# Splitting the keys and queries of a hybrid decoder's attention out of PSUM and stacking them by way of DRAM

## The chip, the cores and the metric

One core of one Trainium2 chip runs the kernel. The metric is the device time of one execution in microseconds, as the median of several runs. A profiled execution gives the trace from which all durations below are read.

## What is computed

One inference step of a decoder trunk of two layers (D_MODEL 1024, 512 prompt rows, and 8 sequences of 4 sample rows against a paged cache). The mixing sub-layer of a layer, cut to what matters:

```python
def hybrid_layer(x, pos, conv_prev, pool_prev, attend, lam_init, p):
    h = rms_norm(x, p['g_mix_pre'])
    z = h @ p['w_in']
    a, ga, u, vb, q, k, v, xd = jnp.split(z, IN_SPLITS, axis=-1)      # 8 x 256 columns
    ya, conv_new = conformer_conv(a, ga, conv_prev, ...)              # 31 taps, LayerNorm, swish
    yb, v_rows = chunk_sgu(gelu(u), gelu(vb), ...)                    # u * (tril(W_s) LN(v) + b)
    o = attend(q, k, v, lam)                                          # softmax 1 - lam * softmax 2
    yc = rms_norm(o, p['attn_sub_g'], LN_EPS) * (1.0 - lam_init)
    yd, pool_new = pool_mix(xd, pool_prev, pos, p['pool_w'], p['pool_scale'])
    x = x + rms_norm(jnp.concatenate([ya, yb, yc, yd], axis=-1) @ p['w_out'], p['g_mix_post'])
    gate, up = jnp.split(rms_norm(x, p['g_ffn_pre']) @ p['w_gu'], 2, axis=-1)
    x = x + rms_norm((silu(gate) * up) @ p['w_down'], p['g_ffn_post'])
    return x, k, v, conv_new, pool_new, v_rows
```

The attention has 4 heads with two softmax maps each (8 maps, 32 dimensions each), a linear position bias per head, and is causal.

## The kernel before

`trunk` runs the two layers one after the other; in each, `mixing` (L348 on) and then the feed-forward part of the prompt, beside which the sample rows' cache attention runs in the background. Every product of the prompt is made from split operands: a float32 value is rounded to a high half, and what is left is the low half; three products (high by high, low by high, high by low) are summed in PSUM.

In `mixing` the input projection has eight column groups of 256, in the order of the list at L395: convolution input, its gate, keys, queries, values, pooling input, u, and the gating's v. A group's 1 MB of raw weights is loaded on SyncE's queue (L198, two buffers); ScalarE casts the high half (`whi`, L190) and VectorE subtracts for the low half (`wlo`, L193). Each group is two features of 128 columns, each feature two halves of the rows: the first 256, and, two steps later, the other 256 and the 32 sample rows. A half is 24 matmuls into the PSUM tile `acc` (two banks), and an eviction by ScalarE. Keys and queries are evicted to `kT` and `qT` (L381); after the second half of the last query feature, `stack` (L459) begins. For each of two chunks `c` (two heads each) it transposes the keys on TensorE for the output, casts the high half on ScalarE (`qkh`, L473) and subtracts on VectorE (`qkl`, L474), and copies pieces of 32 partitions with 12 transfers per stack on SyncE's queue (L478, 48 per layer) into `st_k` and `st_q`. These hold, one under the other, high, low, high of the keys against high, high, low of the queries, so that one matmul of 96 rows makes the three products.

`attention` (L482) is put in after the values. It goes through eight units (row tile i, head hh) in each chunk: two scores matmuls, VectorE's instruction that adds the bias and takes the minimum (L501), ScalarE's exponential with its sum (L503). Three units later come the weights of a unit: a reciprocal (L511), a scaling (L512), the difference of the two maps (L513), transposes on TensorE (L516), their copy (L518), and after each second head the product with the values. Beside it VectorE runs the 60 taps of the convolution (`cacc`, L416), whose norm and transposes (L439, L447, L449) come later. `gating` (L564) begins behind the last eviction: GELU (L586, L587), then per row tile two transposes, statistics and POOL's power for 1/sqrt, the normalised tile (L595) times the gain (L596) plus the bias (L597), then the spatial matmuls and the sum with the spatial bias (L607). `pooling` is at L618. The four results go into the output projection, whose first half of 512 columns starts with the pooling's rows; the second half's weights are cast by ScalarE (L190) behind the last results.

The order on each engine is made when the program is built, by a scheduler that simulates the engines; on the chip each engine and each queue takes its instructions in that order. The tiles `p` (L499, 10 buffers), `t512` (4 buffers) and `y` (4 buffers) are rings.

## Time and profile before

| | us |
|---|---|
| median of 3 runs (lowest to highest) | 1449.32 (1446.21 to 1450.23) |
| the profiled execution | 1448.71 |
| its span | 1446.8 |
| TensorE busy | 1372.0 (95%) |
| VectorE busy | 823.8 (57%) |
| ScalarE busy | 504.7 (35%) |
| GpSimd busy | 262.7 (18%) |

The span is what the trace covers; the execution's own time has 1.9 us around it. PE is TensorE, PEld its weight load, DVE VectorE, ACT ScalarE, POOL GpSimd, SP SyncE. An L number is a line of the kernel. A busy share is an average over stages with different limits, so the rows that follow are read by stage: the mixing of layer 0 lies at about 13 to 192 us, that of layer 1 at about 740 to 907.

### The profile page before, as it was taken

To read this page: it belongs to the slowest core of one execution; us is meant where nothing else is said; L and a number is where in the kernel's file an instruction comes from. 1 tells how busy PE (TensorE), PEld (TensorE's weight loads), DVE (VectorE), ACT (ScalarE), POOL (GpSimd) and SP (SyncE) were. 2 spreads that over 40 slices of the span, in tenths; PEclk is the share of its full clock that TensorE was granted. 3 is DMA by queue.
4 is the path that set the end of the run, shared out by engine and by line. 5 is a ranking of instruction groups with operands and counts; after the bars stand their busy time and mean duration, and the time that the engine had idled before them with its cause. 6 is when DMAs were issued, how large, how long until landed. Compare 5 with 4: busy or idle time off the path is not lost.

```text
span 1446.8 us, 22864 instructions
## 1 busy us (share of the span) xinstructions
PE 1372.0 (95%) x9114; PEld 1078.7 (75%) x9114; DVE 823.8 (57%) x1660; ACT 504.7 (35%) x985; POOL 262.7 (18%) x271
## 2 busy tenths in 40 slices
PE   6999787999999999999989988989999999999997
PEld 6987576877666777777689976777776677768775
DVE  4986759866434333333669976778663333333344
ACT  4346634322224321222343474543322332222231
POOL 1000145455300000000220011544442000000003
PEclk9999799999999999999999997999999999999999
DMA  6452134888848752132434521468877496213132
GB/s 206 116 156 73 59 121 145 301 307 297 296 164 254 241 171 77 59 117 106 150 120 119 146 68 58 163 237 281 318 276 266 153 315 220 81 61 114 59 135 91
DMA packets 160091, 242.15 MB, mean 167 GB/s; under 512 B 10444, under 2 KB 118226, under 8 KB 159986
## 3 DMA queue, kind: packets, MB, share of 16 engines
q1 hardware_dynamic: 141410, 173.32, 37.1%
q0 software_dynamic: 18432, 67.12, 12.4%
q8 instruction: 72, 1.18, 0.3%
q14 instruction: 33, 0.27, 0.1%
q10 hardware_dynamic: 144, 0.26, 0.0%
HBM read 222.33 MB, written 12.04 MB: 162 GB/s over the span
## 4 chain that ended last, share of the span: by engine, by line
PE 81%; DVE 11%; ACT 2%; DMA 2%; issue 2%; POOL 1%; SPq 1%; DVEq 0%; POOLq 0%; ACTq 0%
PE acc L126 61%; PE sx L126 12%; PE ps L126 3%; DVE sca L872 2%; PE s L126 1%; DVE cacc L416 1%; DVE p L501 1%; DVE wlo L193 1%; DVE m L1301 1%; PE oT L126 1%; DVE x_t L1294 1%; ACT whi L190 1%; PE ps L516 1%; SPq L478 1%; PE ps L1001 1%
## 5 line engine op out<-in xcount | busy, mean ns | idle before, releaser
L126 PE MATMUL acc<-xhi,whi 128*128 128x512 f32 (+2 forms) x1152 | 405.5, 353 | 3.2 <-ACT whi L190 2.0
L126 PE MATMUL acc<-xhi,wlo 128*128 128x512 f32 (+2 forms) x1152 | 403.4, 351 | 0.2 <-DVE wlo L193 0.2
L126 PE MATMUL acc<-xlo,whi 128*128 128x512 f32 (+2 forms) x1152 | 402.0, 349 | 1.3 <-DVE xlo L238 1.3
L190 ACT CAST whi<-raw 128x1024 fp32r<-128x1024 f32 x178 | 184.3, 1048 | 333.7 <-PE acc L126 292.8
L193 DVE TENSOR_TENSOR wlo<-raw,whi 128x1024 fp32r<-128x1024 f32 x172 | 217.1, 1268 | 128.7 <-ACT whi L190 126.8
L126 PEld LDWEIGHTS acc<-xhi,whi 128*128 128x128 f32 x1152 | 217.1, 189 | 42.2 <-issue 8.0
L126 PEld LDWEIGHTS acc<-xlo,whi 128*128 128x128 f32 x1152 | 217.2, 189 | 31.9 <-issue 4.1
L126 PEld LDWEIGHTS acc<-xhi,wlo 128*128 128x128 f32 x1152 | 216.9, 188 | 31.5 <-issue 4.7
L126 PE MATMUL acc<-whi,h 128*128 128x512 f32 x704 | 226.7, 397 | 0.0
L126 PEld LDWEIGHTS acc<-whi,h 128*128 128x128 f32 x704 | 131.2, 188 | 44.1 <-issue 11.1
L126 PE MATMUL acc<-wlo,h 128*128 128x512 f32 x352 | 138.6, 395 | 0.0
L1276 POOL TENSOR_TENSOR m<-m,g_g_ffn_post 128x512 f32<-128x512 f32 x14 | 20.1, 1437 | 504.9 <-ACT junk L1275 504.9
L989 DVE STREAM_TRANSPOSE kt<-kr 128x1024 f32<-128x1024 f32 x64 | 78.5, 1233 | 27.6 <-DMA kr<-in_cache_k_dram,ik 23.3
L986 POOL DMA_INDIRECT kr<-in_cache_k_dram,ik x64 | 73.8, 1154 | 100.1 <-DVE kt L989 72.2
L416 DVE SCALAR_TENSOR_TENSOR cacc<-hext,pf,cacc 128x512 f32<-128x512 f32 x120 | 85.4, 747 | 0.6
L1345 DVE SCALAR_TENSOR_TENSOR th<-th,acc 128x512 f32<-128x512 f32 (+1 forms) x46 | 29.9, 649 | 87.2 <-PE acc L126 87.0
L126 PEld LDWEIGHTS acc<-wlo,h 128*128 128x128 f32 x352 | 66.1, 188 | 17.6 <-issue 4.5
L174 POOL TENSOR_TENSOR rsw<-rsw,mhalf 128x1 f32<-128x1 f32 (+2 forms) x62 | 39.1, 636 | 202.9 <-DVE rsw L173 189.4
L1016 POOL DMA_INDIRECT vr<-in_cache_v_dram,iv x64 | 63.2, 988 | 57.0 <-PE sx L126 41.2
L1154 DVE SCALAR_TENSOR_TENSOR sth<-sth,ps 128x64 f32<-128x64 f32 x22 | 4.8, 220 | 86.5 <-ACT sth L1153 86.5
L550 POOL TENSOR_TENSOR rse<-e,mhalf 128x8 f32<-128x8 f32 x4 | 8.5, 2130 | 242.7 <-DVE e L548 242.7
L126 PE MATMUL sx<-vr,pt 128*32 128x256 f32 x512 | 49.3, 381 | 0.0
(401 smaller groups left out, 1864.8 us busy)
## 6 DMA issues: line engine op xcount, KB each, us to landing
raw<-in_w_gu_dram SPq DMA_DIRECT2D x44, 1024.0 KB
raw<-in_w_down_dram SPq DMA_DIRECT2D x20, 1024.0 KB
rws<-in_w_gu_dram SPq DMA_DIRECT2D x40, 512.0 KB
raw<-in_w_in_dram SPq DMA_DIRECT2D x16, 1024.0 KB
raw<-in_w_out_dram SPq DMA_DIRECT2D x8, 1024.0 KB
rwo<-in_w_out_dram SPq DMA_DIRECT2D x16, 512.0 KB
rws<-in_w_down_dram SPq DMA_DIRECT2D x16, 512.0 KB
x<-x_t SPq DMA_DIRECT2D x12, 512.0 KB
```

Of the source, the lines that this page charges most:

```text
L126: T.matmul(out, lhsT, rhs, start=start, stop=stop)
L174: G.tensor_tensor(y, v, mhalf[:P, :n], op=ALU.pow)
L190: S.copy(hi, src)
L193: eng.tensor_tensor(lo, src, hi.bitcast(F32), op=ALU.subtract)
L416: V.scalar_tensor_tensor(a, hext[c][:, t:t + SEQ], pf[:, 8 + 2 * t + c:9 + 2 * t + c], a, op0=ALU.mult, op1=ALU.add)
L478: SY.dma_start(s[32 * g:32 * g + 32, jj, :].bitcast(F32), (hi, lo)[seqs[g]][32 * jj:32 * jj + 32, :].bitcast(F32))
L872: V.scalar_tensor_tensor(a[:, c], ext[:, c, :, t:t + 4], pf[:, 8 + 2 * t + c:9 + 2 * t + c], a[:, c], op0=ALU.mult, op1=ALU.add)
L986: G.indirect_dma_start(out=kr, out_offset=None, in_=ck, in_offset=bass.IndirectOffsetOnAxis(ap=ik[:, s, bg:bg + 1], axis=0))
L989: V.transpose(kt, kr)
L1016: G.indirect_dma_start(out=v.rearrange("p t e -> p (t e)"), out_offset=None, in_=cv, in_offset=bass.IndirectOffsetOnAxis(ap=iv[:, s, a:a + ...
L1276: (V if (t, half) == (3, 1) else G).tensor_tensor(m[t][:, hs], m[t][:, hs], gain[:, hs], op=ALU.mult)
L1345: V.scalar_tensor_tensor(th[:, :n], th[:, :n], 0.5, ou[:, :n], op0=ALU.mult, op1=ALU.mult)
```

## The change

Keys and queries are no longer evicted as float32. `ev_qk` writes the high half straight from PSUM (ScalarE) and the low half from PSUM minus that (VectorE), each as 256 columns, into tiles that live through the stage; the queries' scale is in both. `stack(c)` is called at the end of each query feature: on GpSimd's queue it writes both halves of keys and of queries to DRAM and reads each stack back with three transfers (20 per layer; SyncE's 48 go). The output of the keys (`keys_out`) is made by two matmuls with a rounded identity, one for each half, in place of a transpose. `attention` is put in after the first query feature, with gates: a chunk begins when its queries are done, products with the values when those are done. The reciprocal and the scaling of two heads become one instruction each. In `gating` the gain is applied after the spatial matmuls, and the bias goes through the spatial weights once, in four matmuls, into the spatial bias. The ring of `p` has 8 buffers in place of 10, `t512` 3 in place of 4; two small tiles `cn` use the ring `pt`.

```diff
@@ -36,7 +36,7 @@
 URG = 1000
-PB = 10
+PB = 8
 UL = 3
...
@@ -149,6 +149,8 @@
     ident = cst[:, C_ID:C_ID + 128]
+    identr = cp.tile([128, 128], F32R, name="identr")
+    S.copy(identr, ident)
...
+        SY.dma_start(rows[71:73, :], A["sgu_ln_g"][l].rearrange("(c p) -> c p", p=128))
...
+        V.tensor_copy(pf[:, 77:79], o[:, 71:73])
...
-        kT, kh, kl, qh, ql = {}, {}, {}, {}, {}
+        qk = {(nm, c): [mp.tile([128, SEQ], F32R, name=f"{nm}{c}{s}") for s in "hl"] for nm in "kq" for c in range(2)}
+        pb = mp.tile([128, SEQ], F32, name="pb")
+        SY.dma_start(pb, A["c_pbias"])
+        done = set()
...
-        def ev_tmp(d, c, f, tag):
+        def ev_qk(nm, c, f):
+
             def ev(o, half):
-                if half == 0:
-                    d[c] = mp.tile([128, SEQ], F32, tag="p", bufs=PB, name=tag)
+                hi, lo = qk[nm, c]
                 hs = slice(256 * half, 256 * half + 256)
-                if tag == "kT":
-                    S.copy(d[c][:, hs], o[:, :256])
+                if nm == "k":
+                    S.copy(hi[:, hs], o[:, :256])
+                    V.tensor_tensor(lo[:, hs], o[:, :256], hi[:, hs].bitcast(F32), op=ALU.subtract)
                 else:
-                    S.activation(d[c][:, hs], o[:, :256], AF.Copy, scale=cst[:, C_QS + c:C_QS + c + 1])
+                    sc = cst[:, C_QS + c:C_QS + c + 1]
+                    S.activation(hi[:, hs], o[:, :256], AF.Copy, scale=sc)
+                    V.scalar_tensor_tensor(lo[:, hs], o[:, :256], sc, hi[:, hs].bitcast(F32), op0=ALU.mult, op1=ALU.subtract)
                 if half == 1:
-                    S.activation(zs[:, f, :], o[:, 256:288], AF.Copy, scale=1.0 if tag == "kT" else -QSCALE)
+                    S.activation(zs[:, f, :], o[:, 256:288], AF.Copy, scale=1.0 if nm == "k" else -QSCALE)
             return ev
 
-        qT = {}
         order = [
             (0, [(0, ev_copy(hext[0], 0, 0.5, 30)), (1, ev_copy(hext[1], 1, 0.5, 30))]),
             (256, [(2, ev_ga(0)), (3, ev_ga(1))]),
-            (1280, [(10, ev_tmp(kT, 0, 10, "kT")), (11, ev_tmp(kT, 1, 11, "kT"))]),
-            (1024, [(8, ev_tmp(qT, 0, 8, "qT")), (9, ev_tmp(qT, 1, 9, "qT"))]),
+            (1280, [(10, ev_qk("k", 0, 10)), (11, ev_qk("k", 1, 11))]),
+            (1024, [(8, ev_qk("q", 0, 8)), (9, ev_qk("q", 1, 9))]),
...
-        def stack():
+        def stack(c):
+
+            for nm, seqs in (("k", (0, 1, 0)), ("q", (0, 0, 1))):
+                via = dp.tile([2, 128, SEQ], F32, name=f"via{l}{c}{nm}")
+                for i in range(2):
+                    G.dma_start(via[i], qk[nm, c][i].bitcast(F32))
+                st = ST[nm, c] = yp.tile([128, 4, SEQ], F32R, tag="y", name=f"st_{nm}")
+                for g in range(3):
+                    G.dma_start(st[32 * g:32 * g + 32].bitcast(F32), via[seqs[g]].rearrange("(j p) t -> p j t", p=32))
+
+        def keys_out():
             for c in range(2):
-                st = ST[c] = {}
-
                 o = ps()
                 for t in range(4):
-                    T.transpose(o[:, 128 * t:128 * t + 128], kT[c][:, 128 * t:128 * t + 128], ident)
-                kt = mp.tile([128, 4, 128], F32, tag="t512", bufs=4, name="ktok")
+                    for s in range(2):
+                        mm(o[:, 128 * t:128 * t + 128], qk["k", c][s][:, 128 * t:128 * t + 128], identr, start=(s == 0), stop=(s == 1))
+                kt = mp.tile([128, 4, 128], F32, tag="t512", bufs=3, name="ktok")
                 S.copy(kt, o.rearrange("p (t f) -> p t f", t=4))
                 SY.dma_start(O[2][l, 0].rearrange("(t p) h c d -> p t (h c d)", p=128)[:, :, 128 * c:128 * c + 128], kt)
                 yield
-                for nm, src, seqs in (("k", kT[c], (0, 1, 0)), ("q", qT[c], (0, 0, 1))):
-                    hi = mp.tile([128, SEQ], F32R, tag="t512", bufs=4, name="qkh")
-                    lo = mp.tile([128, SEQ], F32R, tag="t512", bufs=4, name="qkl")
-                    S.copy(hi, src)
-                    V.tensor_tensor(lo, src, hi.bitcast(F32), op=ALU.subtract)
-                    s = yp.tile([128, 4, SEQ], F32R, tag="y", name=f"st_{nm}")
-                    for jj in range(4):
-                        for g in range(3):
-                            SY.dma_start(s[32 * g:32 * g + 32, jj, :].bitcast(F32), (hi, lo)[seqs[g]][32 * jj:32 * jj + 32, :].bitcast(F32))
-                    st[nm] = s
-                    yield
 
         def attention():
-            pb = mp.tile([128, SEQ], F32, tag="pb", name="pb")
-            SY.dma_start(pb, A["c_pbias"])
             y = None
             for c in range(2):
-                st = ST[c]
+                while ("q", c) not in done:
+                    yield
...
-                        mm(sp[:, :W], st["q"][0:96, 2 * hh + m, 128 * i:128 * i + 128], st["k"][0:96, 2 * hh + m, 0:W])
+                        mm(sp[:, :W], ST["q", c][0:96, 2 * hh + m, 128 * i:128 * i + 128], ST["k", c][0:96, 2 * hh + m, 0:W])
...
-                    V.reciprocal(dn[:, 2:3], dn[:, 1:2])
-                    V.tensor_scalar(dn[:, 3:4], dn[:, 0:1], dn[:, 2:3], nlam, op0=ALU.mult, op1=ALU.mult)
+                    if hh == 0:
+                        d2 = den[:, i]
+                        V.reciprocal(d2[:, :, 2:3], d2[:, :, 1:2])
+                        V.scalar_tensor_tensor(d2[:, :, 3:4], d2[:, :, 0:1], nlam, d2[:, :, 2:3], op0=ALU.mult, op1=ALU.mult)
...
                         if hh == 1:
+                            while "v" not in done:
+                                yield
                             values(i)
...
-            gr = mp.tile([128, 2, 256], F32, tag="sgr", name="sgr")
-            SY.dma_start(gr[:, 0, :], A["sgu_ln_g"][l, :].partition_broadcast(128))
-            SY.dma_start(gr[:, 1, :], A["sgu_ln_b"][l, :].partition_broadcast(128))
+            gr = mp.tile([128, 256], F32, tag="sgr", name="sgr")
+            SY.dma_start(gr, A["sgu_ln_b"][l, :].partition_broadcast(128))
...
             SG[l] = (wc, bc)
+            o = acc()
+            for h in range(4):
+                mm(o[64 * (h % 2):64 * (h % 2) + 64, 128 * (h // 2):128 * (h // 2) + 128], gr[:, 64 * h:64 * h + 64], wt[:, h, :])
+            V.tensor_tensor(bsg, o[:, :256].rearrange("p (c t) -> p c t", c=2), bsg, op=ALU.add)
             yield
...
                 V.tensor_scalar(vn[:, t, :], o[:, :256], mean, r, op0=ALU.subtract, op1=ALU.mult)
-                V.tensor_tensor(vn[:, t, :], vn[:, t, :], gr[:, 0, :], op=ALU.mult)
-                V.tensor_tensor(vn[:, t, :], vn[:, t, :], gr[:, 1, :], op=ALU.add)
                 yield
...
-                V.tensor_tensor(t, o.rearrange("p (n t) -> p n t", n=4),
-                                bsg[:, c:c + 1, :].to_broadcast([128, 4, 128]), op=ALU.add)
+                V.scalar_tensor_tensor(t, o.rearrange("p (n t) -> p n t", n=4), pf[:, 77 + c:78 + c],
+                                       bsg[:, c:c + 1, :].to_broadcast([128, 4, 128]), op0=ALU.mult, op1=ALU.add)
...
-                if c0 == 1024 and i == 1:
-                    active.append(stack())
+                if c0 == 1024:
+                    done.add(("q", i))
+                    stack(i)
+                    if i == 0:
+                        active.append(attention())
+                    else:
+                        active.append(keys_out())
                 if i == "v":
-                    active.append(attention())
+                    done.add("v")
```

On VectorE, layer 0, around the first score. L501 (L507 after) is the score's minimum, L416 (L425) a tap into an accumulator `cacc`, L193 (L195) a weight low half, L474 an old low half, L399 a query's new one. Before:

```order
L474 TENSOR_TENSOR qkl<-qT,qkh 128x512
L416 SCALAR_TENSOR_TENSOR cacc_800<-hext_232,pf_82,cacc_800 128x512
L416 SCALAR_TENSOR_TENSOR cacc_442<-hext_231,pf_82,cacc_442 128x512
L416 SCALAR_TENSOR_TENSOR cacc_800<-hext_232,pf_82,cacc_800 128x512
L193 TENSOR_TENSOR wlo<-raw,whi 128x1024
L416 SCALAR_TENSOR_TENSOR cacc_442<-hext_231,pf_82,cacc_442 128x512
L416 SCALAR_TENSOR_TENSOR cacc_800<-hext_232,pf_82,cacc_800 128x512
L501 ISA p,mn<-s,pb 128x128
L501 ISA mn 128x1
```

After:

```order
L425 SCALAR_TENSOR_TENSOR cacc_456<-hext_233,pf_84,cacc_456 128x512
L425 SCALAR_TENSOR_TENSOR cacc_831<-hext_234,pf_84,cacc_831 128x512
L195 TENSOR_TENSOR wlo<-raw,whi 128x1024
L399 SCALAR_TENSOR_TENSOR q1l<-acc,cst,q1h 128x256
L425 SCALAR_TENSOR_TENSOR cacc_831<-hext_234,pf_84,cacc_831 128x512
L507 ISA p,mn<-s,pb 128x128
L507 ISA mn 128x1
```

The first score stands behind nine taps more, and q1l, the other chunk's low half, stands ahead of it too.

On GpSimd's queue, layer 0, from the end of the rows' clearing to the attention norm's power (L550, L560). Before, no transfer stands there:

```order
L356 MEMSET dext_233 128x15
L355 MEMSET hext_232 128x30
L356 MEMSET dext_234 128x15
L550 TENSOR_TENSOR rse<-e_1534,mhalf 128x8
L578 AFFINE_SELECT wt<-wt 128x512
```

After (the eight rows for the keys of chunk 0 and the first of chunk 1 stand ahead of these):

```order
L473 DMA via00q<-q0h 128x512
L476 DMA st_q<-via00q 32x4x512 x2
L476 DMA st_k<-via01k 32x4x512 x2
L473 DMA via00q<-q0l 128x512
L476 DMA st_k<-via01k 32x4x512
L476 DMA st_q<-via00q 32x4x512
L473 DMA via01q<-q1h 128x512
L473 DMA via01q<-q1l 128x512
L476 DMA st_q<-via01q 32x4x512 x3
L560 TENSOR_TENSOR rse<-e_1368,mhalf 128x8
```

The read of chunk 0's query stack stands behind writes and reads of chunk 1's keys, and the last third of it behind the write of q0l.

On TensorE, layer 0, around the last matmul of the input projection (`acc<-xhi,wlo 128x288`). L439 and L447 are transposes of the convolution's norm, L516 (L524) of the attention weights, L575 of the spatial weights, L593 of the gating's v. Before:

```order
L126 MATMUL acc<-xhi,wlo 128x288
L126 MATMUL s<-st_k,st_q 128x384 x2
L575 MATMUL acc<-cst,wn 128x128 x4
L439 MATMUL ps<-cst,cacc_442 128x128
L439 MATMUL ps<-cst,cacc_800 128x128
L126 MATMUL s<-st_k,st_q 128x384 x2
L593 MATMUL acc<-cst,uv 128x128 x4
L126 MATMUL s<-st_k,st_q 128x512 x2
L439 MATMUL ps<-cst,cacc_442 128x128
```

After, where the last 96 matmuls of the projection begin at the end of these rows:

```order
L126 MATMUL s<-st_k,st_q 128x512
L126 MATMUL oT<-pt,vtok 64x128
L524 MATMUL ps<-cst,p 128x128 x2
L448 MATMUL ps<-cst,cacc_456 128x128
L448 MATMUL ps<-cst,cacc_831 128x128
L126 MATMUL oT<-pt,vtok 64x128
L126 MATMUL s<-st_k,st_q 128x512
L448 MATMUL ps<-cst,cacc_456 128x128
L448 MATMUL ps<-cst,cacc_831 128x128
L524 MATMUL ps<-cst,p 128x128 x2
L126 MATMUL acc<-wn,pw 128x512
L126 MATMUL acc<-xhi,whi 128x256
```

Chunk 1's widest scores were behind the projection's last matmul and are ahead of its last 96 now.

## Rows read from the trace of the kernel before

**Rows 1.** The page's head: the span and its instructions.

```profile
span 1446.8 us, 22864 instructions
```

**Rows 2.** Layer 0 windows: us, busy PE, PEld, DVE, ACT, POOL; PEclk, DMA share, GB/s.

```profile
40.40:81.00 40.60, 38.92 (x306) 38.21 (x304) 38.75 (x57) 14.09 (x30) 0.00 (x0) 1.00 0.41 116
81.00:130.00 49.00, 45.29 (x325) 40.05 (x325) 43.79 (x120) 27.55 (x77) 0.00 (x0) 0.97 0.42 122
130.00:145.00 15.00, 15.00 (x124) 14.69 (x124) 5.31 (x12) 9.05 (x16) 2.66 (x1) 1.00 0.27 88
145.00:175.30 30.30, 19.48 (x125) 13.58 (x123) 23.67 (x79) 21.36 (x42) 6.91 (x9) 0.66 0.20 68
175.30:190.00 14.70, 13.21 (x66) 10.80 (x64) 5.96 (x12) 4.32 (x7) 2.70 (x4) 1.00 0.01 5
```

**Rows 3.** The same of layer 1's tail.

```profile
862.00:889.60 27.60, 20.13 (x112) 13.53 (x112) 22.81 (x77) 18.53 (x39) 5.09 (x9) 0.63 0.21 74
889.60:905.00 15.40, 13.91 (x80) 11.49 (x76) 6.02 (x12) 4.50 (x7) 2.60 (x4) 1.00 0.02 7
```

**Rows 4.** DVE groups, layer 0: shapes xcount | busy us, mean ns | idle.

```profile
L416 DVE SCALAR_TENSOR_TENSOR cacc<-hext,pf,cacc 128x512 f32<-128x512 f32 x60 | 42.6, 747 | 0.3
L193 DVE TENSOR_TENSOR wlo<-raw,whi 128x1024 fp32r<-128x1024 f32 x16 | 19.8, 1237 | 8.5 <-ACT whi L190 8.4
L512 DVE TENSOR_SCALAR den<-den,lam 128x1 f32<-128x1 f32 x16 | 4.0, 266 | 0.1
L511 DVE RECIPROCAL den<-den 128x1 f32<-128x1 f32 x16 | 2.4, 157 | 5.9 <-ACT p L503 5.9
L595 DVE TENSOR_SCALAR vn<-acc,ag,rsw 128x256 f32<-128x256 f32 x4 | 2.1, 538 | 0.0
L597 DVE TENSOR_TENSOR vn<-vn,sgr 128x256 f32<-128x256 f32 x4 | 1.7, 417 | 0.1
L474 DVE TENSOR_TENSOR qkl<-kT,qkh 128x512 fp32r<-128x512 f32 x2 | 1.4, 688 | 0.7 <-DMA st_q<-qkh 0.7
```

**Rows 5.** DVE timeline (start us, us): eleven taps, and each layer's first score.

```profile
65.40 7.37 DVE L416 SCALAR_TENSOR_TENSOR cacc<-hext,pf,cacc 128x512 f32<-128x512 f32 x11
...
81.05 0.29 DVE L501 CUSTOM_DVE_ANT_0 p<-s,pb 128x128 f32<-128x128 f32 x1 [0.21 <-PE s L126]
...
800.35 0.28 DVE L501 CUSTOM_DVE_ANT_0 p<-s,pb 128x128 f32<-128x128 f32 x1
```

**Rows 6.** Gathered cache keys, 512 KB each: issue ns min/median/max; landing.

```profile
L986 POOL DMA_INDIRECT kr<-in_cache_k_dram,ik x64: 933/941/1936, 252.2 to 1086.2; - x64
...
DMA to landing us min/median/max: 4.2/6.5/9.8
```

**Rows 7.** Query stack: issue ns; PE's waits (us, times, longest); scores.

```profile
L478 SPq DMA_DIRECT2D st_q<-qkh x32: 507/588/1712, 74.3 to 819.0; - x32
...
PE s L126 <- DMA st_q<-qkl: 0.9, 2, 0.7
...
L126 PE MATMUL s<-st_k,st_q 96*128 96x384 f32 x8 | 2.7, 374 | 1.5 <-DVE mn L501 1.4
...
L126 PE MATMUL s<-st_k,st_q 96*128 96x512 f32 x8 | 4.5, 628 | 0.0
```

**Rows 8.** PE timeline: each layer's last projection matmul, output projection's second half.

```profile
144.71 0.29 PE L126 MATMUL acc<-xhi,wlo 128*128 128x288 f32 x1
...
192.29 0.50 PE L126 MATMUL acc<-whi,yd 128*128 128x512 f32 x1 [2.13 <-ACT whi L190]
...
861.56 0.30 PE L126 MATMUL acc<-xhi,wlo 128*128 128x288 f32 x1
...
907.40 0.61 PE L126 MATMUL acc<-whi,yd 128*128 128x512 f32 x1 [2.15 <-ACT whi L190]
```

**Rows 9.** ACT, 130 to 193: table loads (group), weight casts (timeline).

```profile
L503 ACT ACT_TABLE_LOAD x3 | 3.8, 1283 | 0.1
...
188.36 3.88 ACT L190 CAST whi<-raw 128x1024 fp32r<-128x1024 f32 x4
```

More of the change, by code (lines that the diff above doesn't have):

```diff
@@ L277, in params @@
         lam_init = 0.8 - 0.6 * math.exp(-0.3 * l)
-        rows = tp.tile([72, 128], F32, tag="prow", name="prow")
+        rows = tp.tile([74, 128], F32, tag="prow", name="prow")
         for i, n in enumerate(("conv_b", "conv_ln_g", "conv_ln_b", "pool_scale")):
@@ L564, in gating @@
         def gating():
-            wn = mp.tile([128, 4, 128], F32, tag="t512", bufs=4, name="wn")
+            wn = mp.tile([128, 4, 128], F32, tag="t512", bufs=3, name="wn")
             SY.dma_start(wn, A["sgu_w"][l].rearrange("h t s -> t h s"))
```

14 lines of the change are left out of this document (7 added, 7 removed).

## The prediction

> **What bounds the kernel now.** I read the span first [rows 1], then busy time by stage of each mixing sub-layer [rows 2, 3], then VectorE (DVE) by groups and in order of time [rows 4, 5], then the transfers and what waits for them [rows 6, 7], and last the two ends that matter on TensorE (PE) and ScalarE (ACT) [rows 8, 9]. Only the two mixing sub-layers change, some 170 us each. Their middle has three parts. From the gated convolution input to the first attention score (40.4 to 81.0 in layer 0) PE and DVE are both full: 38.9 and 38.8 of 40.6 us [rows 2]. From there to the last matmul of the input projection (145.0, [rows 8]) PE is still nearly full (45.3 of 49.0, then 15.0 of 15.0). Then comes a tail in which nobody is full: from 145.0 to 175.3 PE is busy 19.5 of 30.3 us and its granted clock is 0.66, between its two levels; DVE is busy 23.7 and ACT 21.4. The tail ends when the second half of the output projection starts, at 192.29 in layer 0 and 907.40 in layer 1: 47.3 and 45.5 us after the last projection matmul (144.71 + 0.29; 861.56 + 0.30) [rows 8]. So DVE limits the first part, PE the second, and a chain through ACT, DVE and PE the third.
>
> **The first part gets longer.** In DVE's order the first score now stands behind 50 of the 60 convolution taps in layer 0 and 53 in layer 1, not 41, and behind all eight low-half instructions of keys and queries, where two were. DVE had no slack there, so each of these counts. A tap costs 0.67 us start to start (7.37 us for 11, [rows 5]): 9 x 0.67 = 6.0 us in layer 0, 12 x 0.67 = 8.0 in layer 1. A low half is now a 128x256 instruction that reads PSUM, eight times. The nearest rows are 0.54 us (128x256 from PSUM, L595) and 0.42 (two SBUF operands, L597), and as a lower bound half of the old 128x512 one, 0.34 [rows 4]; I take 0.48, so 8 x 0.48 = 3.8 us (2.8 to 4.3), less the two old ones that stood before the score, 2 x 0.69 = 1.4. Sum: first score **+8.4 us in layer 0 (81.05 to 89.5), +10.4 in layer 1 (800.35 to 810.8)**. ACT's side only gets lighter (the high half is now the copy out of PSUM itself, four casts of 128x512 go); it was busy 14 of 40.6 us, so I price that at nothing.
>
> **The transfers.** 48 copies on SyncE's (SP's) queue go, at 0.588 us of issue each, 28 us per layer [rows 7]. PE waited in the whole front half for these copies twice, 0.9 us in all [rows 7], and for no weight load; what hides the issues is that weights are loaded two tiles ahead. Price 0 (a gain of 0.9 at most). In their place stand 20 transfers of 256 KB on GpSimd's (POOL's) queue, each read behind its write. POOL is idle there (0.00 busy in the first two stretches, [rows 2]) and nothing else of the mixing is queued behind them before the attention norm's power, which ran after 130 us. The path that counts is the last query half of chunk 0: between it and the score stand 13 taps, a weight low half (1.24, [rows 4]) and one low half more, 13 x 0.67 + 1.24 + 0.48 = 10.4 us, so DVE finishes it at 89.5 - 10.4 = 79.1. Then come issue, write, issue, read. No such transfer is in the trace; the nearest is POOL's gather of 512 KB: 0.94 us to issue, 4.2 / 6.5 / 9.8 us to landing (least, median, most, [rows 6]). Halves of 256 KB with plain rows should be near the least: 79.1 + 2 x (0.94 + 4.2) = 89.4, just before DVE gets to the score at 89.5. At the median 94.0, at the most 100.6. I take the least, and keep the others for the rivals. The Trainium skill, "DMA: Bandwidth & Descriptors", section "Anatomy of one DMA — SWDGE (gpsimd) path", gives about 2.0 us plus bytes over 436 GB/s, an estimate of 2.6 us for such a transfer, and says that the receipt of a write to DRAM is the heaviest; by it the stack would be there well before DVE. The trace's least landing of twice the bytes, 4.2 us, is not far from that, its median is.
>
> The same page, section "Issuing engines are not separate DMA queues", speaks against the move: another issuing engine saves only the time of issuing. The rows above agree, in that PE waits for no weight.
>
> **The second part.** From the first score to the last projection matmul PE has the same dense matmuls in both orders. Chunk 1's eight widest scores (four of 384 columns, four of 512) stood behind the last dense one in both layers and stand before it now: 4 x 0.374 + 4 x 0.628 = 4.0 us ([rows 7]; 3.0 if all were as the narrower), and with them four transposes of the convolution's norm, 4 x 0.13 = 0.5. The keys' 16 product matmuls in place of 8 transposes: 306 dense matmuls in 38.9 us are 0.127 each at twice the columns [rows 2], so eight more are 0.5 to 1.0; I take 0.8. Against that stand the 3.7 us in which PE idled from 81 to 130; with fewer taps between the scores I let 3 of them go (0 to 3.7). Net +2.3. Last dense matmul: 145.0 + 8.4 + 2.3 = **155.7** in layer 0; 861.9 + 10.4 + 2.3 = **874.6** in layer 1.
>
> **The tail gets shorter.** DVE's work from first score to 190 was 43.8 + 5.3 + 23.7 + 6.0 = 78.8 us [rows 2]. Of that 9 x 0.75 = 6.7 has moved ahead. The sixteen reciprocals and scalings, 16 x (0.157 + 0.266) = 6.8, become eight of each kind on two heads at about the same duration, 3.4: -3.4. The eight gain and bias steps of 0.42 (L597 and its twin) go, -3.3, and one 128x256 addition comes, +0.4. Two old low halves go, -1.4. Left: 78.8 - 6.7 - 3.4 - 2.9 - 1.4 = 64.4. Between first score and last dense matmul DVE worked 49.1 of 64 us, 0.77; over the new 66.2 us (89.5 to 155.7) that is 50.8, so 13.6 us are left for the tail, where 23.7 + 6.0 = 29.7 were: **-16.1**. Of what is taken out of the tail, chunk 1's scores, exponentials and weights, which stood ahead of the gating on both engines, are the larger part. ACT also had table loads of 1.283 us each in it [rows 9], because the exact GELU alternated with the exponentials: 6 in layer 0's mixing and 4 in layer 1's, one in each after: -6.4 and -3.8. If all of both is on the path, the tail is 47.3 - 16.1 - 6.4 = 24.8 in layer 0; with the table loads hidden, 31.2. For layer 1 (28.8 us of DVE in its tail, [rows 3]; the same removals) 45.5 - 16.1 - 3.8 = 25.6, or 29.4. What is late next is the gating: last eviction, GELU, then four transposed tiles, each through statistics and POOL's power, the spatial matmuls, the product, and on ACT the cast of the result ahead of four weight casts (3.88 us, [rows 9]) that the second output half waits for. Adding that chain up in the new order from rows of the same kind gives 27.5 us, inside both pairs of bounds, and I take it for both. The fold's four extra matmuls (under 1 us) lie where PE idles. Second half of the output projection: 155.7 + 27.5 = **183.2** (192.3 before, -9.1) and 874.6 + 27.5 = **902.1** (907.4, -5.3).
>
> PE will idle some 8 and 10 us in gaps before the first score. In the tail before, where PE was busy 64% of the time, the granted clock was 0.66 [rows 2]; if the gaps do the same to about 10 us of matmuls, a quarter of that is lost in all: +2.5 for both layers (0 to 6). Sum: -9.1 - 5.3 + 2.5 = -11.9 on the profiled 1448.71 us (span 1446.8, the rest lies around it), 1436.8; that run is 0.6 below the median of the runs, so **1437.4**.
>
> **The rivals.**
> 1. *A larger gain.* The gating's chain overlaps more: tail 20 us instead of 27.5, -15 in all, **1422.4**. For it: DVE has only 13.6 us of work left in 27.5. Against: the chain of four tiles through POOL is serial, and the last tile's transposes now stand behind 19 matmuls of the output projection.
> 2. *Landing at the median.* The first score comes 4.5 us later than DVE could take it (94.0), in each layer: **1446.4**, which can no longer be told from no change. DVE takes its instructions in order, so the taps behind that score wait too, and nothing is won back.
> 3. *Both a median landing and a tail whose table loads were hidden* (31 us, so 3.5 more each): 1446.4 + 7 = **1453.4**, still no change that can be measured.
> 4. *Slower: the way through DRAM decides.* Weight loads keep the DMA engines 41% busy in this stretch [rows 2] and the writes and reads are in one POOL queue, each read waiting for its write with the next writes behind it. At landings of 9.8 us, the most in [rows 6], the first score is at 100.6, 11.1 later than in the sum, and 2 x 11.1 = 22.2 more gives **1459.6**. It decides from the point where the added wait per layer passes the gain, 11.9 / 2 = 6 us: a first score later than about 95.5.
> 5. *The change doesn't do what it says:* the queue that it relieves held nobody up. That I have priced in; the gain then comes from attention's earlier place and the lighter DVE alone.
>
> **How the numbers follow.** Forecast (1430 to 1444) 0.41; larger gain 0.13; median landing 0.11; both 0.13; slower 0.22. About 0.3% (4.3 us) is what a measurement of this kernel can tell from no change: faster is below 1445, slower above 1453.7. Rivals 2 and 3 lie between, and the forecast and the first rival below: faster 0.54, same 0.24, slower 0.22. The range reaches from the larger gain to the slow case, 1421 to 1460; cases beyond either end are left some 0.2 in all.
>
> **What would show it.** Right: the first score at about 89 and 811, released by DVE and not by a DMA; the last projection matmul near 156 and 875; one table load in each mixing; the second output half near 183 and 902; transfers on POOL's queue that land in 4 to 5 us; gaps on PE at 74 to 89 ended by DVE's weight low halves. Wrong: PE or DVE waiting at the first score for the read of the query stack (rivals 2 and 4); the tail still above 40 us, with DVE idle in it, which would mean that the chain and not the work set it; or SP's relief showing as earlier weights.

## The result and the profile after

The changed kernel takes 1470.86 us (median of 4 runs, 1470.22 to 1471.66) against 1449.76 for the kernel before (four runs now; 1449.32 was the median of the first three): a ratio of 1.0155, with an interval of 1.0137 to 1.0174. It is 1.5% slower where 0.8% faster was forecast, and it lies outside the range, whose upper end was 1460.

The page's head and the windows of the changed kernel follow, cut where the prediction cut them: from the convolution's start to the first score, from there to the last projection matmul, from there to the output projection's second half. Columns are as in [rows 2]; layer 0 comes first, then layer 1.

```profile
span 1468.5 us, 22838 instructions
...
40.40:90.20 49.80, 39.86 (x294) 38.60 (x292) 45.42 (x70) 11.82 (x25) 9.64 (x17) 0.93 0.54 154
90.20:167.80 77.60, 70.50 (x496) 62.56 (x496) 53.95 (x151) 42.60 (x116) 5.53 (x8) 0.91 0.26 83
167.80:195.10 27.30, 24.53 (x163) 19.04 (x162) 17.89 (x37) 15.19 (x25) 10.71 (x10) 0.94 0.27 83
...
764.30:814.20 49.90, 40.76 (x296) 39.49 (x295) 47.69 (x71) 11.83 (x25) 9.49 (x17) 0.93 0.53 149
814.20:892.00 77.80, 71.44 (x499) 62.90 (x499) 51.57 (x148) 42.63 (x116) 5.50 (x8) 0.91 0.28 86
892.00:922.30 30.30, 25.00 (x161) 19.52 (x159) 19.35 (x37) 15.86 (x27) 11.41 (x10) 0.89 0.35 112
```

The same cut of the kernel before:

```profile
41.20:81.00 39.80, 38.12 (x299) 37.41 (x298) 37.95 (x54) 14.09 (x30) 0.00 (x0) 1.00 0.42 118
81.00:145.00 64.00, 60.29 (x447) 54.75 (x447) 49.10 (x131) 36.60 (x93) 2.66 (x1) 0.97 0.39 114
145.00:192.30 47.30, 32.85 (x190) 24.39 (x188) 30.60 (x91) 27.98 (x51) 11.91 (x14) 0.78 0.16 51
...
760.40:800.40 40.00, 38.61 (x304) 37.90 (x302) 38.18 (x53) 14.09 (x30) 0.00 (x0) 1.00 0.42 119
800.40:861.90 61.50, 58.05 (x447) 53.51 (x448) 49.36 (x133) 36.33 (x93) 2.56 (x1) 1.00 0.40 118
861.90:907.40 45.50, 34.39 (x189) 25.12 (x187) 29.89 (x90) 25.43 (x49) 10.09 (x14) 0.77 0.15 53
```

| us more than before | layer 0 | layer 1 | forecast, 0 / 1 |
|---|---|---|---|
| first part, to the first score | +10.0 | +9.9 | +8.4 / +10.4 |
| second part, to the last projection matmul | +13.6 | +16.3 | +2.3 / +2.3 |
| tail, to the output projection's second half | -20.0 | -15.2 | -19.8 / -18.0 |
| from there to the feed-forward's first gated product | -1.9 | -0.6 | 0 |
| feed-forward to the next layer, or to the end | +3.0 | +7.4 | 0 |

With the start 0.8 us earlier the column sums to the +21.7 of the spans. PE was idle 19.9 us of layer 0's three parts before (1.7, 3.7, 14.5) and is idle 19.8 after (9.9, 7.1, 2.8): the tail's idle time was emptied, and as much of it stands in the two parts ahead.

PE's waits that carry this: the first score of each layer, the last projection matmul, the first matmul of the output projection's second half (start us, us, what ended the idle time before it).

```profile
89.68 0.66 PE L126 MATMUL s<-st_k,st_q 96*128 96x128 f32 x2 [4.73 <-DMA st_q<-via00q]
...
167.46 0.29 PE L126 MATMUL acc<-xhi,wlo 128*128 128x288 f32 x1
...
195.14 0.40 PE L126 MATMUL acc<-whi,yd 128*128 128x512 f32 x1
...
813.77 0.61 PE L126 MATMUL s<-st_k,st_q 96*128 96x128 f32 x2 [1.89 <-issue]
...
891.70 0.30 PE L126 MATMUL acc<-xhi,wlo 128*128 128x288 f32 x1
...
922.30 0.40 PE L126 MATMUL acc<-whi,yd 128*128 128x512 f32 x1
```

They answer to [rows 8]. In layer 1 the profile puts the wait down to "issue", but the read of the last part of the query stack is issued on GpSimd's queue at 805.97 and lands 7.7 us later, at 813.7, just before the score starts. So in both layers the first score came with that read. DVE (the last low half of chunk 0's queries, then twelve taps, then the first score) and POOL's queue (the write of that half, the read behind it) over the same time in layer 0, and last the read of layer 1:

```profile
76.34 0.47 DVE L399 SCALAR_TENSOR_TENSOR q0l<-acc,cst,q0h 128x256 fp32r<-128x256 f32 x1
76.73 8.03 DVE L425 SCALAR_TENSOR_TENSOR cacc<-hext,pf,cacc 128x512 f32<-128x512 f32 x12
...
90.16 0.29 DVE L507 CUSTOM_DVE_ANT_0 p<-s,pb 128x128 f32<-128x128 f32 x1 [3.21 <-PE s L126]
```

```profile
79.76 0.56 POOL L473 DMA_DIRECT2D via00q<-q0l  x1
80.31 0.56 POOL L476 DMA_DIRECT2D st_k<-via01k  x1
85.61 0.55 POOL L476 DMA_DIRECT2D st_q<-via00q  x1 [4.74 <-DMA via00q<-q0l]
...
805.97 0.55 POOL L476 DMA_DIRECT2D st_q<-via10q  x1
```

The half is done at 76.8, but its write is issued only at 79.76, behind a read of q0h that waited for its own write; it lands before 85.61, and the read is in at 89.7. That is 12.9 us from the finished half to the score on PE, and DVE waits 3.21 us of them. In layer 1 it is 11.4 us (802.4 to 813.8), and DVE waits 0.56.

Where the second part grew: busy time of PE in it, by tile, layer 0, before and after (the columns after the length are PE and PEld, then the other engines that touch the tile). First `acc`, `s` and `ps` before:

```profile
81.00:145.00 64.00, 48.84 (x340) 44.07 (x340) 0.00 (x0) 7.03 (x21) 0.97 0.39 114
...
81.00:145.00 64.00, 6.88 (x25) 4.22 (x25) 15.23 (x35) 0.00 (x0) 0.97 0.39 114
...
81.00:145.00 64.00, 6.43 (x42) 4.88 (x42) 0.76 (x2) 3.73 (x9) 0.97 0.39 114
```

The same three after:

```profile
90.20:167.80 77.60, 51.52 (x341) 46.37 (x342) 0.00 (x0) 7.02 (x21) 0.91 0.26 83
...
90.20:167.80 77.60, 10.65 (x31) 5.67 (x30) 19.91 (x43) 0.00 (x0) 0.91 0.26 83
...
90.20:167.80 77.60, 12.53 (x72) 9.58 (x72) 4.58 (x10) 6.27 (x16) 0.91 0.26 83
```

The dense matmuls (`acc`) are as many, but take 2.7 us more at the lower granted clock (0.91 for 0.97); scores take 3.8 us more, transposes and other small products (`ps`) 6.1 us more (72 for 42), products with the values 1.1 us more (52 for 40). Matmuls of different tiles overlap, so these add up to more than the 10.2 us by which PE's busy time grows. Its idle time grows from 3.7 to 7.1.

### The profile page after: what moved, and what is told of

Its sections match the earlier page's. It is cut to its first block, busy times and chain, and to the rows that moved or that the text cites. A ratio compares the mean times of both kernels' runs of the same rounds, so it can differ in the third digit from the quotient of the medians.

```text
span 1468.5 us, 22838 instructions
## 1 busy us (share of the span) xinstructions
PE 1385.7 (94%) x9146; PEld 1090.9 (74%) x9146; DVE 819.2 (56%) x1624; ACT 491.1 (33%) x972; POOL 279.2 (19%) x311
## 4 chain that ended last, share of the span: by engine, by line
PE 77%; DVE 11%; DMA 4%; issue 4%; ACT 2%; POOL 2%; SPq 0%; DVEq 0%; POOLq 0%; ACTq 0%
PE acc L126 59%; PE sx L126 11%; PE ps L126 3%; DVE sca L888 2%; DVE cacc L425 2%; DVE wlo L195 2%; PE s L126 1%; DMA kr<-in_cache_k_dram,ik 1%; DVE m L1317 1%; DVE x_t L1310 1%; PE oT L126 1%; ACT whi L192 1%; PE ps L1017 1%; PE ps L524 1%; PE ps L237 1%
## 5 line engine op out<-in xcount | busy, mean ns | idle before, releaser
L126 PE MATMUL acc<-xhi,whi 128*128 128x512 f32 (+2 forms) x1152 | 410.2, 357 | 6.5 <-ACT whi L192 3.2
L126 PE MATMUL acc<-xhi,wlo 128*128 128x512 f32 (+2 forms) x1152 | 407.7, 354 | 4.0 <-DVE wlo L195 4.0
L126 PE MATMUL acc<-xlo,whi 128*128 128x512 f32 (+2 forms) x1152 | 406.6, 353 | 1.1 <-DVE xlo L240 1.1
L195 DVE TENSOR_TENSOR wlo<-raw,whi 128x1024 fp32r<-128x1024 f32 x172 | 216.4, 1264 | 151.6 <-ACT whi L192 138.3
L126 PEld LDWEIGHTS acc<-xhi,whi 128*128 128x128 f32 x1152 | 222.0, 193 | 47.3 <-issue 8.7
L126 PEld LDWEIGHTS acc<-xhi,wlo 128*128 128x128 f32 x1152 | 221.9, 193 | 35.4 <-issue 4.9
L126 PEld LDWEIGHTS acc<-xlo,whi 128*128 128x128 f32 x1152 | 221.7, 192 | 32.7 <-issue 4.8
L425 DVE SCALAR_TENSOR_TENSOR cacc<-hext,pf,cacc 128x512 f32<-128x512 f32 x120 | 84.2, 744 | 0.8
L126 PE MATMUL sx<-kt,qs 128*32 128x128 f32 x1024 | 45.2, 281 | 0.2 <-DVE kt L1005 0.2
```

The lines of the kernel that those rows point to most:

```text
L126: T.matmul(out, lhsT, rhs, start=start, stop=stop)
L195: eng.tensor_tensor(lo, src, hi.bitcast(F32), op=ALU.subtract)
L425: V.scalar_tensor_tensor(a, hext[c][:, t:t + SEQ], pf[:, 8 + 2 * t + c:9 + 2 * t + c], a, op0=ALU.mult, op1=ALU.add)
```

## The experiments

All ratios are to the kernel before, run on the same chip.

**Run e1** asks why the last 96 projection matmuls stand behind chunk 1. In the trace of the changed kernel the pooling's second product is the last thing ahead of them, and its additions on DVE (L643) stand behind the last score:

```profile
147.63 1.38 DVE L643 TENSOR_TENSOR wn<-s 64x512 f32<-64x512 f32 x2
```

```profile
149.85 0.69 PE L448 MATMUL ps<-cst,cacc 128*128 128x128 f32 x2 [3.44 <-DVE xn L450]
151.16 0.69 PE L524 MATMUL ps<-cst,p 128*128 128x128 f32 x2 [0.62 <-DVE xn L450]
151.64 1.91 PE L126 MATMUL acc<-wn,pw 128*128 128x512 f32 x2
152.56 1.20 PE L126 MATMUL acc<-xhi,whi 128*128 128x256 f32 x1
```

```diff
-                o = acc()
+                o = ps()
                 mm(o, pw[:, c, :], wn[:, 0:SEQ])
```

> The changed kernel with one edit: the pooling's product goes to the PSUM ring of the small tiles (ps, three buffers) instead of the ring that the input projection uses (acc, two buffers). Theory A (the pooling's tile stands in the projection's ring, its VectorE additions stand behind chunk 1's scores, so the last 96 projection matmuls wait for it): the last projection matmul comes back from 167.9 to 155-159 in layer 0 and from 892 to 876-882 in layer 1, no idle of TensorE over 1 us between 135 and 155, and the time is 1446-1458. Theory B (the chain of chunk 1's scores itself, in TensorE's order, holds the projection up): the ends stay within 3 us of 167.9 and 892, the time at 1466-1472. Theory C (the longer first part, first score at 90 and 814, is the loss): time stays over 1464 too.

1485.64 us, ratio 1.0211 (1.0174 to 1.0248). The three windows of layer 0:

```profile
40.60:91.90 51.30, 39.85 (x294) 38.58 (x292) 45.40 (x70) 11.82 (x25) 9.66 (x17) 0.92 0.56 157
91.90:152.30 60.40, 60.30 (x459) 56.80 (x458) 41.08 (x113) 36.51 (x98) 3.33 (x4) 0.95 0.32 99
152.30:198.30 46.00, 33.36 (x198) 24.06 (x198) 28.84 (x75) 24.32 (x46) 10.85 (x14) 0.89 0.12 39
```

Theory A's place is right: with the tile elsewhere PE is idle 0.1 us in the second part, which ends at 152.3 instead of 167.8. Its price is wrong: the tail is 46.0 us again, and the kernel is no faster (1.0211 where the changed kernel had 1.0155; the two intervals just touch). The wait on the pooling is real, and what it held back was not the limit; attention's rest, now behind the projection, took the time back.

**Run e2** puts attention where it was, with all else as changed.

```diff
-                    if i == 0:
-                        active.append(attention())
-                    else:
+                    if i == 1:
                         active.append(keys_out())
                 if i == "v":
                     done.add("v")
+                    active.append(attention())
```

> The changed kernel with attention put in after the values, as before, everything else of the change kept (halves from PSUM, way through DRAM, batched reciprocals, folded gain and bias). Theory A (attention's earlier place pushes the pooling's additions back on VectorE): chunk 1's scores are again among and behind the last projection matmuls, the last of them comes at 150-158 in layer 0, time 1440-1456. Theory C (the way through DRAM and the eight low halves in the first part cost the time): the first part is as long as in the changed kernel, time 1462-1472.

1471.81 us, ratio 1.0124 (1.0087 to 1.0162). The first score comes at 100.8 and 816.3. The early place is not the cause of the loss; the rest of the change is about as slow without it (the interval overlaps that of the changed kernel, 1.0137 to 1.0174).

**Runs e3 and e4** make two small edits in the kernel before: the fold of gain and bias with the batched reciprocals (their hunks of the change), and e1's edit.

> The kernel before with only the batched reciprocals and the folded gain and bias of the gating: some 6.3 us less of VectorE's work per layer, all of it between the first score and the output projection. If VectorE's work sets the tail: 1436-1444. If the gating's chain through ScalarE and GpSimd sets it: 1445-1451.

> The kernel before with the pooling's product in the ring of the small tiles. Before, the pooling was done at 129, ahead of the last 96 projection matmuls, and TensorE idled 3.7 us from 81 to 130. Theory A expects a small effect here, 1443-1451; a gain over 8 us would mean that the ring was already the limit before.

e3: 1450.83 us, ratio 0.998 (0.9963 to 0.9997). e4: 1449.44 us, ratio 0.9971 (0.9953 to 0.9989). Both are worth a little. DVE's removed work, some 6 us per layer, buys 1 to 1.5 us in each (0.2% of the kernel), as expected where a chain sets the tail and not DVE's work.

**Runs e5, e6 and e7** take the change apart. e5 is the changed kernel with direct copies; e6 is the kernel before with attention's early place alone; e7 is the kernel before with the way through DRAM alone.

The edit of e5, in `stack(c)` of the changed kernel (e7 makes the opposite one in the kernel before):

```diff
-                via = dp.tile([2, 128, SEQ], F32, name=f"via{l}{c}{nm}")
-                for i in range(2):
-                    G.dma_start(via[i], qk[nm, c][i].bitcast(F32))
                 st = ST[nm, c] = yp.tile([128, 4, SEQ], F32R, tag="y", name=f"st_{nm}")
-                for g in range(3):
-                    G.dma_start(st[32 * g:32 * g + 32].bitcast(F32), via[seqs[g]].rearrange("(j p) t -> p j t", p=32))
+                for jj in range(4):
+                    for g in range(3):
+                        SY.dma_start(st[32 * g:32 * g + 32, jj, :].bitcast(F32), qk[nm, c][seqs[g]][32 * jj:32 * jj + 32, :].bitcast(F32))
```

The edit of e6, in the kernel before, cut to where the parts are put in; the gates in `stack` and `attention` are those of the change:

```diff
-                if c0 == 1024 and i == 1:
-                    active.append(stack())
+                if c0 == 1024:
+                    active.append(stack(i))
+                    if i == 0:
+                        active.append(attention())
                 if i == "v":
-                    active.append(attention())
+                    done.add("v")
```

> The changed kernel with the stacks filled by 48 direct copies on SyncE's queue again, from the new halves, no way through DRAM and nothing on GpSimd's queue; all else as changed. Theory D (the first part's new idle of TensorE, 8 us per layer, comes from the way through DRAM and is not won back): first score at 81-86 in layer 0, TensorE's idle before it under 4 us, time 1452-1463. Theory E (what the first part loses the second would have lost, TensorE's work and idle are only moved): 1466-1473. If SyncE's issues delayed the weights, TensorE would wait for weight halves before 81 and the time would be above 1473.

> The kernel before with only attention's place changed: the stack is made chunk by chunk (old copies on SyncE's queue, from the old evictions), attention is put in after the first query feature, with the same gates. In its order all of chunk 1's scores stand ahead of the last 96 projection matmuls, as in the changed kernel, and the table loads fall from 11 to 5. Theory F (the early place only moves TensorE's work and idle from the tail into the second part): the last projection matmul 8-15 us later in layer 0 than the 145.0 of before, the tail from there to the output projection's second half 28-38 instead of 47.3, time 1443-1456. If the early place is by itself what made the changed kernel slow: over 1460. If it is a gain that something else ate: under 1440.

> The kernel before with only the way of the stacks changed: two writes to DRAM and three reads for each on GpSimd's queue in place of twelve copies on SyncE's. In its order the first score stands behind 52 taps instead of 41 and behind 54 more projection matmuls. Theory D: the first score comes at 88-96 instead of 81.05 and the time is 1453-1466. If the way through DRAM is hidden (attention has slack there): 1446-1452.

e5: 1459.15 us, ratio 1.0023 (1.0010 to 1.0036). e6: 1443.11 us, ratio 0.9918 (0.9897 to 0.9939). e7: 1467.45 us, ratio 1.0080 (1.0058 to 1.0102). The three windows of e6 in layer 0:

```profile
41.00:80.70 39.70, 38.12 (x299) 37.40 (x298) 37.98 (x54) 14.07 (x30) 0.00 (x0) 1.00 0.42 119
80.70:158.10 77.40, 67.82 (x474) 59.78 (x475) 62.84 (x178) 41.93 (x115) 4.70 (x5) 0.93 0.32 94
158.10:183.30 25.20, 23.13 (x162) 17.93 (x161) 18.12 (x43) 14.96 (x25) 8.75 (x10) 1.00 0.34 107
```

The early place alone does to the second part and the tail what the whole change does (+13.4 and -22.1), and leaves the first part as it was (39.7): a gain of 0.8%. The 1443.11 us are just inside theory F's range, but on this chip the kernel before took 1455.15; at 1449.76 the ratio gives 1437.9, under the 1440 that was to mean a gain that something else ate. The tail, 25.2, is shorter than theory F's 28 to 38 too. In the changed kernel the early place gains nothing (e2), so its worth depends on the rest.

In e5 the first part is 41.7 us in place of 49.8; in e7 the first score moves from 81.05 to 92.75 (its time is above theory D's range, but its ratio, 1461 us at 1449.76, inside it). In e5 the same half and the first score it serves stand on DVE so:

```profile
76.96 0.48 DVE L399 SCALAR_TENSOR_TENSOR q0l<-acc,cst,q0h 128x256 fp32r<-128x256 f32 x1
77.36 5.39 DVE L425 SCALAR_TENSOR_TENSOR cacc<-hext,pf,cacc 128x512 f32<-128x512 f32 x8
82.65 0.29 DVE L505 CUSTOM_DVE_ANT_0 p<-s,pb 128x128 f32<-128x128 f32 x1
```

With direct copies DVE is at the score 5.2 us after the half is done (13.4 us by way of DRAM, 12.9 to the score on PE). So the way through DRAM is what makes the first part long. Every kernel here that goes through DRAM does so on GpSimd's queue; whether the DRAM or that queue costs the time was not tried apart.

**Runs e8, e9 and e12** look for the best version.

> The kernel before with the two edits that were measured apart: batched reciprocals with folded gain and bias (ratio 0.998) and the pooling's product in the ring of small tiles (ratio 0.997). If their gains add: 0.994-0.996 of before, some 1441-1444 where before is 1450. If both relieve the same wait: 0.997.

> The kernel before with attention's early place and chunk-wise stacks (0.992 alone) and the batched reciprocals and folded gain and bias (0.998 alone); stacks by SyncE's direct copies from old evictions. If the two add: 0.988-0.991. If the fold's saved work lay in the tail that the early place has already emptied: 0.991-0.994. It is also the version that should beat both kernels.

> The early place and fold, and the pooling's product in the ring of small tiles. With the changed kernel that edit moved the projection's last matmuls 16 us ahead and attention's end 16 us back, and lost. If the same happens here: 0.995-1.005 and a tail over 40 us. If the loss there came from the long first part: 0.984-0.989.

e8: 1449.06 us, ratio 0.9955 (0.9936 to 0.9974), which is what adding gives; that both relieve the same wait (0.997) is still inside the interval. e9: 1445.96 us, 0.9934 (0.9910 to 0.9958): the fold adds nothing to the early place. e12: 1449.69 us, 0.9958 (0.9945 to 0.9971): as with e1, moving the pooling's tile makes the tail 50 us long and costs.

**Runs e10, e11, e13 and e14** add single parts to the early place: the way through DRAM; the fold and smaller rings; to e11 the keys' output by products; to e11 the queries' halves out of PSUM.

> The kernel before with attention's early place and with the way through DRAM on GpSimd's queue, no halves from PSUM, no fold. Theory D (the way through DRAM costs 6 to 10 us per layer before the first score): first score at 91-95 in layer 0, ratio 1.000-1.010, that is 12 to 25 us slower than the early place with direct copies. If DRAM only hurts together with the new halves: under 0.996.

> The early place and fold with the changed kernel's smaller rings (8 buffers for the attention's maps instead of 10, 3 instead of 4 for the 512-column tiles), old evictions and direct copies. What then still separates it from the changed kernel with direct copies (1.0023) is the halves split out of PSUM and the keys' output by products. If the rings are what costs: 0.997-1.003. If not: within 0.002 of the early place with fold.

> The early place, fold and smaller rings of e11 (0.9933), and the keys' output made by products of the split halves with a rounded identity, as in the changed kernel, instead of transposes. If these products are what still separates e11 from the changed kernel with direct copies (1.0023): 0.998-1.003. If not: 0.992-0.996.

> The early place, fold and smaller rings of e11 (0.9933), and the queries' halves split straight out of PSUM (four low halves of 128x256 per layer instead of two of 128x512), the keys as before. If the split out of PSUM is the rest (VectorE full before the first score, TensorE waiting for weight low halves): about half of 0.9%, 0.996-1.000, with TensorE waiting 1.5 us or more for weight low halves before the first score. If not: 0.992-0.995.

e10: 1455.13 us, 0.9989 (0.9976 to 1.0002), first score at 93.0, as theory D had it, at a price a little under its 12 us. e11: 1445.96 us, 0.9933 (0.9912 to 0.9954). e13: 1443.57 us on a chip on which the kernel before took 1448.16, 0.9964 (0.9952 to 0.9977). e14: 1448.66 us, 1.0003 (0.9988 to 1.0018). The rings cost nothing. The way through DRAM costs 0.7% here too, on top of e6. The queries' halves cost 0.7% on top of e11, a clear step and a little more than expected, though PE's waits for weight low halves before the first score are only 0.8 and 1.2 us, less than expected: more of it is in the second part (79.9 and 81.6 us, 78.3 and 78.5 in e11). The profile of e14 is of the shortest of its runs (1443.31), so it shows only a part of that step. The keys' products cost some 0.3%, between the two ranges expected; the intervals of e13 and e11 just overlap, so this may be nothing. The keys' halves were not tried alone.

**Runs s1 to s4** put the four steps on one chip.

> The changed kernel, on the same chip as the next three, since ratios to the kernel before moved by up to 0.4% from chip to chip. Expected 1.5% above before.

> The changed kernel with direct copies on SyncE's queue. If the way through DRAM is the largest loss on one and the same chip too: 12 to 20 us under the changed kernel. If the difference was one of chips: under 6.

> Early place, fold and small rings, with the old evictions and keys by transposes. If halves from PSUM and keys by products cost something together: 8 to 14 us under s2. If that was chips: under 4.

> The kernel before with the early place alone. If fold and rings are worth nothing on top: within 3 us of s3. Against the kernel before: 8 to 13 us faster.

| | us | ratio (interval) | step |
|---|---|---|---|
| kernel before | 1447.89 | | |
| s4: early place alone | 1436.65 | 0.9920 (0.9899 to 0.9941) | -11.2 |
| s3: and fold, reciprocals, smaller rings | 1438.23 | 0.9939 (0.9914 to 0.9963) | +1.6 |
| s2: and halves out of PSUM, keys by products | 1452.14 | 1.0025 (1.0011 to 1.0039) | +13.9 |
| s1: and the way through DRAM, the change | 1471.02 | 1.0162 (1.0138 to 1.0186) | +18.9 |

The ratios are within 0.0007 of those on the other chips (0.9918, 0.9933, 1.0023, 1.0155), so the concern about chips in these expectations was needless. The early place alone beats both kernels: 0.8% under the kernel before and 2.3% under the changed one. The first windows of s2, then s4, in layer 0, show where the two costs begin:

```profile
41.80:83.40 41.60, 36.81 (x286) 35.75 (x285) 40.45 (x63) 10.20 (x22) 0.00 (x0) 1.00 0.39 110
```

```profile
39.60:79.30 39.70, 38.07 (x299) 37.36 (x297) 37.90 (x54) 14.04 (x30) 0.00 (x0) 1.00 0.42 119
```

The first part is 39.7 us with the early place, 41.6 with the halves, 50.1 with the way through DRAM (s1); in layer 1 39.9, 43.4 and 49.7. That is some 5 us of the step of 13.9 and 15 us of the step of 18.9; the second parts hold another 5 us of the former (80.0 in both layers, 77.8 and 77.4 in s3), and layer 1's feed-forward 7 us of the latter.

## Why the prediction was wrong

**The first part was right in size, and its cause half right.** The first score was forecast 8.4 and 10.4 us later and came, counted from the start of the part (the times forecast for layer 1 leave out what layer 0 was to gain), 10.0 and 9.9 later. Low halves measured 0.47 us (q) and 0.42 (k), where 0.48 was taken. But five of the nine added taps in layer 0, and seven of the twelve in layer 1, stood ahead of the score only with the way through DRAM: with direct copies (e5) 45 and 46 taps stand there, for 50 and 53, and the first part is only 1.9 and 3.4 us longer than before. DVE's busy time in the part grew by 7.5 and 9.5 us, so the work was counted about right; why it stood there was not. I charged the whole delay to DVE's order as given and called the transfers hidden, so the price of the way through DRAM was booked under another name. PE and DVE also waited for it outright (4.73 and 3.21 us in layer 0, 1.89 and 0.56 in layer 1); rival 4's mechanism was there, at a first score of 90.2, not the 95.5 from which it was said to decide.

**The transfers were nearly right one by one.** Landings for the writes to DRAM and for the reads back into the stacks:

```profile
DMA to landing us min/median/max: 2.3/2.5/6.7
...
DMA to landing us min/median/max: 3.1/4.3/7.7
```

The 0.94 + 4.2 us taken for each hop from [rows 6] compare with 0.56 of issue and these, which count from the start of the issue. In layer 0 the half was ready 2.3 us earlier than forecast and the score came 0.7 later, because the hops stand in one queue in which each read waits for its write with the next write behind it. The write that counted took 5.6 us, with three key reads around it, and in layer 1 the read that counted took 7.7, the longest of all, behind three key reads and two of its own stack. The estimate of 2.6 us that the Trainium skill's fit gives for a transfer of this size ("DMA: Bandwidth & Descriptors", "Anatomy of one DMA — SWDGE (gpsimd) path") agrees with the writes' median of 2.5 and not with these two.

**The step that failed is the second part, "Net +2.3".** It measured +13.6 and +16.3. The working let PE's busy time grow by 5.3 us and its idle time shrink by 3.0; busy time grew by 10.2 and 13.4, and idle time grew too, by 3.4 and 2.9. The scores were nearly right (4.0 forecast, 3.8 measured). In layer 0 there are 49 more instructions, where the working had 20. Missing was the rest of chunk 1's work that goes with the scores on PE: 9 transposes of its weights and 12 products with the values. The keys' 16 products were booked less 8 transposes, but those had stood in the first part before (47 to 65 us). The small products alone grew by 6.1 us where 1.3 were counted, and the dense matmuls took 2.7 us more at the lower clock in layer 0 alone, where 2.5 was set aside for both layers. The idle time was let go for fewer taps between the scores, with no row behind it; its largest piece now is PE's 3.44 us wait for DVE just ahead of the pooling's last product, and in e1, where the pooling's tile is elsewhere and attention's rest comes later, it is 0.1 us. What is missing in the second part is 11.3 and 14.0 us, 25 of the 34 us between forecast and result.

**The tail was right** (27.3 and 30.3 us, 27.5 forecast), and so was its reason: chunk 1 left it. e6 shows the same with 25.2 us. Since the tail was given its relief in full and the second part only a sixth of the load, the two together were priced at 16 to 17.5 us of gain per layer; the early place, which does the same to both, brings 5.6 (s4, 11.2 in two layers).

**The feed-forward was priced at nothing and cost 10.4 us.** In layer 1 the first and the third stretch of 15 us from the first gated product on show a part of it, before and then after:

```profile
957.80:972.80 15.00, 12.98 (x110) 12.79 (x111) 9.14 (x20) 4.96 (x13) 10.16 (x12) 1.00 0.73 265
...
987.80:1002.80 15.00, 15.00 (x190) 11.05 (x179) 14.06 (x28) 6.01 (x10) 7.06 (x6) 1.00 0.79 256
```

```profile
972.10:987.10 15.00, 13.14 (x96) 12.96 (x97) 7.68 (x18) 4.87 (x13) 9.97 (x12) 0.89 0.69 259
1002.10:1017.10 15.00, 12.49 (x130) 8.98 (x132) 10.24 (x22) 5.67 (x9) 5.60 (x5) 0.94 0.70 232
```

PE gets 96 matmuls done for 110, at a granted clock of 0.89 for 1.00, and then 130 for 190. Between the two the gather of cached keys on GpSimd's queue waits once for DVE:

```profile
POOL kr L1002 <- DVE nn L984: 9.1, 1, 9.1
```

This wait is in all six profiles with the way through DRAM (the changed kernel, s1, e1, e2, e7, e10), and they take 495.3 to 496.6 us from the first gated product to the end. In the fourteen others the gather waits 0.3 us at most for that instruction, and that stretch is 488.5 to 494.9 us. On one and the same chip the former take 1.7 to 8.1 us more than the latter. So this loss goes with the way through DRAM. The code there is untouched, but its order was made anew, and I read the order of the mixing alone; why it comes out so, and whether the wait is what costs the time, was not tried. Layer 0's +3.0 is open: this stretch is 514 to 519 us in every kernel run here, the faster ones too, against 512.4 in the profile of before.

**The rivals.** Rival 5 was true as far as it went: no run shows a gain from taking 48 issues off SyncE's queue, and e5, which puts them back and leaves DRAM out, is faster by 1.3%. The Trainium skill's rule that another issuing engine saves only the issuing ("DMA: Bandwidth & Descriptors", "Issuing engines are not separate DMA queues") agrees with that. Both median landings and a longer tail (rival 3) did not come about.

## What to carry over

When work is moved from an idle stretch into a full one, count all that is moved, on each engine, and let the full stretch pay for it; here the tail's gain and the second part's loss were nearly the same work, and only the difference was a gain. A delay that the order shows is still caused by something: ask what the order was waiting for before booking it to the engine on which it appears. And a change of three parts is best priced part by part: here, in the order of the steps, one was worth -0.8%, and the other two cost 0.9% and 1.3%. Such prices hold only beside the other parts: the way through DRAM cost 0.8% in the kernel before (e7), 0.7% with the early place (e10) and 1.3% on top of all else, and without the early place the changed kernel is no slower (e2).

## What the runs showed of the hardware

Eight writes of 256 KB per layer from GpSimd's queue landed 2.5 us after the start of their issue in the median, and 6.7 us at most (86.15 to 92.85). The one that decided layer 0's first score took 5.6 us, with two key reads issued just ahead of it and one behind, in a part in which the DMA engines were 0.54 busy.

Reads of 256 KB issued on that queue 0.55 us apart landed more than twice as far apart: six of them stand in a row in layer 1 from 803.2 on, and the first three landed 4.1, 4.8 and 5.6 us after the start of their issue, the last two 7.0 and 7.7 (the landing of the fourth is not in the trace). That is 1.2 to 1.3 us apart, with the DMA engines 0.53 busy in this part.
